# Where in SBUF the operands of the split-float matmuls start: taking a 64-byte pad out

## The chip, the cores and the metric

The kernel runs on one NeuronCore of a Trainium2 chip. The metric is the device time of one execution in microseconds. Three runs of the kernel before gave 1196.93, 1199.04 and 1201.48 us, so its median is 1199.04 us.

## The reference, cut to what matters

One decoder layer over 256 tokens of width 2048, batch 1, everything in float32:

```python
mod = silu(c) @ w_ada + b_ada                      # 2048 x 12288, six vectors of 2048
h = rms_norm(x, g) * (1 + scale_m) + shift_m
proj = h @ w_in                                    # 2048 x 5648: q, k, v, xs, z, B, C, dt
mix = concat(rms_norm(attention(q, k, v)), ssd(xs, z, B, C, dt)) @ w_out
x = x + gate_m * mix
h = rms_norm(x, g2) * (1 + scale_f) + shift_f
u = causal_dwconv(h @ w_up)                        # 2048 x 11264
x = x + gate_f * ((silu(u_g) * u_val) @ w_down)    # 5632 x 2048
return rms_norm(x, g3)
```

Attention is causal within one block of 256 tokens, with a bias per head and distance; the SSD part is one chunk of 256.

## The kernel before, in words

**Split floats.** Every large product is made of three float32r matmuls. A float32 number is kept as a high part (rounded to float32r) and a low part (the rest). `mm3` (L276 to L279) adds high x high, high x low and low x high. The tile of 128 x 128 weights is the operand that is loaded into TensorE (stationary), and the activations of 256 tokens stream past it: 256 columns, once the high half `a[:, 0:T]`, once the low half `a[:, T:2*T]`. Each matmul has its own weight load in front of it, so the program is one long sequence of pairs of a weight load and a matmul. The V projection (`v_unit`, L348) is turned round: there the activations are loaded and the weights stream, in pieces of 352, 352 and 336 columns.

**Weights.** SyncE's queue brings about 1 MB of weights at a time into a slot `s_...` of the pool `ws` (8320 bytes per partition a slot). `hi_lo_part` (L255 to L260) then makes two pieces of it: ScalarE writes the high part into a slot of the pool `wh` (L258), VectorE the low part into a slot of the pool `wl` (L259). Each of these pools has four slots of 4224 bytes. A unit of 2048 columns is two pieces of 1024, that is two runs of eight blocks, each block used by three matmuls.

**Activations.** What streams lies in `hT` (16 tiles of 2 x 256 numbers, for the input projection, tile names hT), `cat` and `cats` (for the output projection), `h2` (for the up projection, shown as h) and `gT` (for the down projection, shown as g). All are split floats, made by `hilo` or `ada_norm`.

**Stages.** Up to about 455 us: the modulation vectors (`ada`, partly on VectorE at L210, partly as float32 matmuls at L217 that lie between the others), the input projection (wa), attention, SSD (L557 to L562 are its small float32r matmuls, tile sg) and the output projection (oa). Their order is written out by hand in `ORDER`. After that the feed-forward: up projection over the first half of the contraction (u1a), then the second half (u2a) with the convolution and gate, down projection (da), then the other half of the columns (ua, da), and the last norm. In the feed-forward TensorE has nothing but `mm3`, except for a few matmuls at the end.

**Placement.** The pools are laid out in SBUF one behind the other in the order in which they are opened: `const`, `ws`, `pad0`, `wh`, `wl`, `pad1`, `tmp`, `xres`, `mix`, and so on. A pad is a pool with one tile of 16 floats, 64 bytes per partition, that nothing uses:

```python
    mkpool("pad0").tile([P, 16], F32, name="pad0")
    whp = mkpool("wh", 4)
    wlp = mkpool("wl", 4)
    mkpool("pad1").tile([P, 16], F32, name="pad1")
    tp = mkpool("tmp", 2)
```

Since 8320 is 65 x 128 and 4224 is 33 x 128, all slots of a pool start at the same place within 128 bytes, and the four slots of `wh` and of `wl` start in turn at 0 and 128 within 256 bytes.

Of the kernel before, what the change touches and what calls it, by code (L numbers as in the profile page):

```python
# [10 lines left out]
F32 = mybir.dt.float32  # L11
# [5 lines left out]
P = 128  # L17
# [77 lines left out]
def hymba_layer(ctx, tc, xT, c_row, cT, w_ada, vecs, consts, relb, onehot, w_vdt, w_in, w_out, w_up1, w_up, w_dn, outT):  # L95
# [3 lines left out]
    def mkpool(name, bufs=1, **kw):  # L99
        return ctx.enter_context(tc.tile_pool(name=name, bufs=bufs, **kw))  # L100
# [4 lines left out]
    mkpool("pad0").tile([P, 16], F32, name="pad0")  # L105
    whp = mkpool("wh", 4)
    wlp = mkpool("wl", 4)
    mkpool("pad1").tile([P, 16], F32, name="pad1")
    tp = mkpool("tmp", 2)
    xp = mkpool("xres")  # L110
    psp = mkpool("psum", 5, space=bass.MemoryType.PSUM)
# [805 lines left out]
```

## Time and profile before

| | |
|---|---|
| three runs | 1196.93, 1199.04, 1201.48 us |
| the profiled execution | 1196.57 us, span 1194.8 us |
| TensorE matmul busy | 1167.5 us, 98% of the span |
| TensorE weight load busy | 1113.3 us, 93% |
| VectorE, ScalarE busy | 915.0 us, 636.9 us |
| mean granted TensorE clock | 0.988 |
| read from HBM | 306 MB, 258 GB/s over the span |

Matmuls overlap each other in the records: one is shown as lasting 0.28 us although the next one starts after 0.11 us. So the rate of TensorE is read from the distance between the starts of neighbouring matmuls, called the gap here, or from how many of them a stretch of time holds.

### The profile page before, as it was taken

The page shows a single profiled execution, that of the slowest core. Times are in us where ns is not written, and L with a number is a line of the kernel's source. Part 1 is how long each engine was busy: PE and PEld are TensorE (multiplying, and loading weights), DVE is VectorE, ACT ScalarE, POOL GpSimd, SP SyncE. Part 2 cuts the span into 40 slices and gives each one's busy share as a digit, 9 for nine tenths or more (in the row PEclk, how much of TensorE's full clock was granted, in tenths as well). Part 3 has the DMA queues.
Part 4 walks back from the last instruction along what each step waited for, and adds up shares of the span by engine and source line. Part 5 has one row for each costly group of instructions (what it writes and reads, how often), then busy time and mean ns, then how long its engine had stood idle before and what let it go on. Part 6 is the DMA issues. An engine that isn't in the chain of part 4 may idle for free.

```text
span 1194.8 us, 23406 instructions
## 1 busy us (share of the span) xinstructions
PE 1167.5 (98%) x9760; PEld 1113.3 (93%) x9760; DVE 915.0 (77%) x1371; ACT 636.9 (53%) x959; POOL 0.9 (0%) x7
## 2 busy tenths in 40 slices
PE   6999999999999999999999999999999999999996
PEld 3899989988878898999999999999999999999995
DVE  6889979987988798786599984446888889656554
ACT  4544434457786544446567654444555555555552
POOL 0000000000000000000000000000000000000000
PEclk8899999999999999999999999999999999999998
DMA  9989988776765996997565545558878776545552
GB/s 359 409 338 337 327 335 304 276 268 246 287 242 214 365 383 237 343 357 245 183 204 186 201 146 194 195 194 276 295 299 301 284 282 227 196 150 196 194 194 96
DMA packets 47444, 309.60 MB, mean 259 GB/s; under 512 B 5568, under 2 KB 6761, under 8 KB 16105
## 3 DMA queue, kind: packets, MB, share of 16 engines
q1 hardware_dynamic: 46170, 307.04, 70.6%
q8 instruction: 76, 1.25, 0.4%
q10 hardware_dynamic: 1168, 1.06, 0.4%
q14 instruction: 30, 0.25, 0.1%
HBM read 305.98 MB, written 2.11 MB: 258 GB/s over the span
## 4 chain that ended last, share of the span: by engine, by line
PE 96%; DVE 1%; DMA 1%; ACT 1%; SPq 0%; issue 0%; DVEq 0%; ACTq 0%
PE ua L278 7%; PE ua L279 7%; PE da L279 7%; PE da L278 7%; PE da L277 7%; PE ua L277 7%; PE wa L277 6%; PE wa L279 6%; PE wa L278 6%; PE va L348 4%; PE u1a L278 3%; PE u1a L279 3%; PE u1a L277 3%; PE u2a L277 3%; PE u2a L279 3%; PE u2a L278 3%
## 5 line engine op out<-in xcount | busy, mean ns | idle before, releaser
L258 ACT CAST h_u<-s_u 128x1024 fp32r<-128x1024 f32 x176 | 183.6, 1050 | 188.3 <-PE ua L278 95.2
L259 DVE TENSOR_TENSOR l_u<-s_u,h_u 128x1024 fp32r<-128x1024 f32 x176 | 213.4, 1223 | 66.6 <-ACT h_u L258 64.6
L277 PE MATMUL ua<-h,h_u 128*128 128x256 f32 x704 | 194.3, 276 | 0.0
L278 PE MATMUL ua<-h,h_u 128*128 128x256 f32 x704 | 194.3, 276 | 0.0
L279 PE MATMUL ua<-h,l_u 128*128 128x256 f32 x704 | 194.3, 276 | 0.0
L279 PE MATMUL da<-g,l_d 128*128 128x256 f32 x704 | 194.3, 276 | 0.0
L278 PE MATMUL da<-g,h_d 128*128 128x256 f32 x704 | 194.3, 276 | 0.0
L277 PE MATMUL da<-g,h_d 128*128 128x256 f32 x704 | 194.1, 276 | 0.0
L259 DVE TENSOR_TENSOR l_d<-s_d,h_d 128x1024 fp32r<-128x1024 f32 (+1 forms) x128 | 108.8, 888 | 83.6 <-ACT h_d L258 83.6
L277 PE MATMUL wa<-hT,h_w 128*128 128x256 f32 x576 | 162.1, 282 | 0.8 <-ACT h_w L258 0.8
L279 PE MATMUL wa<-hT,l_w 128*128 128x256 f32 x576 | 159.8, 279 | 0.0
L278 PE MATMUL wa<-hT,h_w 128*128 128x256 f32 x576 | 159.7, 278 | 0.0
L258 ACT CAST h_d<-s_d 128x1024 fp32r<-128x1024 f32 (+1 forms) x128 | 98.2, 782 | 115.0 <-PE da L278 104.3
L210 DVE SCALAR_TENSOR_TENSOR ada<-ada,cb 128x2048 f32<-128x2048 f32 x60 | 137.2, 2288 | 11.5 <-DMA ada<-w_ada 11.2
L279 PEld LDWEIGHTS da<-g,l_d 128*128 128x128 f32 x704 | 132.2, 188 | 0.0
L277 PEld LDWEIGHTS ua<-h,h_u 128*128 128x128 f32 x704 | 132.2, 188 | 0.0
L278 PEld LDWEIGHTS ua<-h,h_u 128*128 128x128 f32 x704 | 132.2, 188 | 0.0
L279 PEld LDWEIGHTS ua<-h,l_u 128*128 128x128 f32 x704 | 132.2, 188 | 0.0
L278 PEld LDWEIGHTS da<-g,h_d 128*128 128x128 f32 x704 | 132.2, 188 | 0.0
L277 PEld LDWEIGHTS da<-g,h_d 128*128 128x128 f32 x704 | 132.1, 188 | 0.0
L258 ACT CAST h_w<-s_w 128x1024 fp32r<-128x1024 f32 x72 | 73.7, 1048 | 88.3 <-PE wa L278 42.7
L277 PEld LDWEIGHTS wa<-hT,h_w 128*128 128x128 f32 x576 | 108.4, 188 | 11.3 <-ACT h_w L258 3.6
(236 smaller groups left out, 2689.4 us busy)
## 6 DMA issues: line engine op xcount, KB each, us to landing
ada<-w_ada SPq DMA_DIRECT2D x96, 1024.0 KB, 6.1
s_u<-w_up SPq DMA_DIRECT2D x88, 1024.0 KB, 5.0
s_d<-w_dn SPq DMA_DIRECT2D x64, 704.0 KB, 4.1
s_w<-w_in SPq DMA_DIRECT2D x36, 1024.0 KB, 7.1
s_o<-w_out SPq DMA_DIRECT2D x16, 1024.0 KB, 8.3
s_v<-w_vdt SPq DMA_DIRECT2D x8, 1040.0 KB, 6.6
x<-xT SPq DMA_DIRECT2D x4, 512.0 KB, 4.8
outT<-x SPq DMA_DIRECT2D x2, 640.0 KB, 3.0
```

The lines of the kernel that those rows point to most:

```text
L210: dve.scalar_tensor_tensor(ws[:, :D], ws[:, :D], 1.0, cb, op0=ALU.mult, op1=ALU.mult, accum_out=mod[:, j:j + 1])
L258: act.copy(wh[:, :m], ws[:, o:o + m])
L259: dve.tensor_sub(wl[:, :m], ws[:, o:o + m], wh[:, :m].bitcast(F32))
L277: pe.matmul(o, whs, a[:, 0:T], start=first, stop=False)
L278: pe.matmul(o, whs, a[:, T:2 * T], start=False, stop=False)
L279: pe.matmul(o, wls, a[:, 0:T], start=False, stop=last)
L348: pe.matmul(va[tt][i][:, :n], lo if st == 2 else hi, (wl if st == 1 else wh)[:, s], start=f and st == 0, stop=l and st == 2)
```

## The change

The pool `pad1` is no longer opened. Everything opened after it moves down by 64 bytes per partition; everything before it stays. No instruction is added, removed or moved: on each engine the built program has the same instructions on the same tiles in the same order.

```diff
     mkpool("pad0").tile([P, 16], F32, name="pad0")
     whp = mkpool("wh", 4)
     wlp = mkpool("wl", 4)
-    mkpool("pad1").tile([P, 16], F32, name="pad1")
     tp = mkpool("tmp", 2)
     xp = mkpool("xres")
```

Where the tiles start in the built program, in bytes of a partition, with the rest after division by 256 in brackets:

| tiles | before | after |
|---|---|---|
| slots of wh | 60672 (0), 64896 (128), 69120 (0), 73344 (128) | the same |
| slots of wl | 77568 (0), 81792 (128), 86016 (0), 90240 (128) | the same |
| three slots of ws | 35648 (64), 43968 (192), 52288 (64) | the same |
| tri_r and ones_r, loaded for sg | 33216 (192), 33728 (192) | the same |
| hT, first tile | 137536 (64) | 137472 (0) |
| cat, cats, first tiles | 170304 (64), 137536 (64) | 170240 (0), 137472 (0) |
| h2 | 125248 (64) | 125184 (0) |
| gT, first tile | 174400 (64) | 174336 (0) |
| am, streams for sg | 153920 (64) | 153856 (0) |
| x, and the first scratch tile of tmp | 108864 (64), 94528 (64) | 108800 (0), 94464 (0) |
| ada and s slots beside ws, first | 203200 (192) | 203136 (128) |

The tiles within hT, cat, cats, h2 and gT are steps of 2048 bytes with two halves of 1024, so each of their streams starts at the same rest.

## Rows read from the trace of the kernel before

**Rows 1.** The page's part 1: busy time, share of the span, instructions.

```profile
PE 1167.5 (98%) x9760; PEld 1113.3 (93%) x9760; DVE 915.0 (77%) x1371; ACT 636.9 (53%) x959; POOL 0.9 (0%) x7
```

**Rows 2.** The page's part 4: shares of the chain that ended last.

```profile
PE 96%; DVE 1%; DMA 1%; ACT 1%; SPq 0%; issue 0%; DVEq 0%; ACTq 0%
```

**Rows 3.** Stretches: PE, PEld, DVE, ACT, POOL busy, PEclk, DMA share, GB/s.

```profile
36.90:100.00 63.10, 62.27 (x513) 58.02 (x512) 54.75 (x81) 35.02 (x50) 0.00 (x0) 1.00 0.94 364
100.00:228.00 128.00, 128.00 (x1044) 123.35 (x1044) 113.86 (x153) 51.08 (x56) 0.00 (x0) 1.00 0.86 313
228.00:454.70 226.70, 225.99 (x1770) 193.36 (x1772) 186.77 (x376) 141.70 (x271) 0.00 (x0) 1.00 0.74 283
464.20:465.30 1.10, 1.10 (x7) 1.10 (x7) 1.10 (x1) 0.00 (x0) 0.00 (x0) 0.50 0.41 171
588.60:1088.60 500.00, 500.00 (x4414) 500.00 (x4413) 381.70 (x548) 279.69 (x402) 0.00 (x0) 1.00 0.65 225
```

**Rows 4.** Groups of matmuls of L277 by shape; L278 and L279 have the same counts.

```profile
L277 PE MATMUL ua<-h,h_u 128*128 128x256 f32 x704 | 194.3, 276 | 0.0
...
L277 PE MATMUL da<-g,h_d 128*128 128x256 f32 x704 | 194.1, 276 | 0.0
L277 PE MATMUL wa<-hT,h_w 128*128 128x256 f32 x576 | 162.1, 282 | 0.8 <-ACT h_w L258 0.8
...
L277 PE MATMUL u2a<-h,h_u 128*128 128x256 f32 x352 | 97.2, 276 | 0.0
...
L277 PE MATMUL u1a<-h,h_u 128*128 128x256 f32 x352 | 96.5, 278 | 0.7 <-ACT h L313 0.7
...
L277 PE MATMUL oa<-cat,h_o 128*128 128x256 f32 x128 | 36.6, 286 | 0.0
...
L277 PE MATMUL oa<-cats,h_o 128*128 128x256 f32 x128 | 35.8, 280 | 0.0
```

**Rows 5.** TensorE in order of time, 36 to 1182 us: start, lasting (us).

```profile
36.89 0.31 PE L277 MATMUL wa<-hT,h_w 128*128 128x256 f32 x1
...
588.69 0.28 PE L277 MATMUL u2a<-h,h_u 128*128 128x256 f32 x1
...
1088.49 0.28 PE L277 MATMUL da<-g,h_d 128*128 128x256 f32 x1
...
1181.54 0.28 PE L279 MATMUL da<-g,l_d 128*128 128x256 f32 x1
```

**Rows 6.** TensorE in order of time, 156 to 160 us, around a stretch of wide gaps.

```profile
156.24 0.61 PE L217 MATMUL adp<-ada,c 128*32 128x512 f32 x4
156.79 0.39 PE L277 MATMUL wa<-hT,h_w 128*128 128x256 f32 x1
157.01 0.28 PE L278 MATMUL wa<-hT,h_w 128*128 128x256 f32 x1
...
159.49 0.28 PE L278 MATMUL wa<-hT,h_w 128*128 128x256 f32 x1
159.60 0.28 PE L279 MATMUL wa<-hT,l_w 128*128 128x256 f32 x1
159.72 0.28 PE L277 MATMUL wa<-hT,h_w 128*128 128x256 f32 x1
159.83 0.28 PE L278 MATMUL wa<-hT,h_w 128*128 128x256 f32 x1
```

**Rows 7.** The chain that ended last, a piece of the V projection.

```profile
170.43 11.40 PE va L348 x72
```

**Rows 8.** TensorE in order of time, SSD's matmuls.

```profile
350.94 0.28 PE L559 MATMUL sg<-am,ones_r 128*128 128x256 f32 x1
...
351.41 0.28 PE L277 MATMUL oa<-cat,h_o 128*128 128x256 f32 x1
```

**Rows 9.** TensorE in order of time, start of the feed-forward, at the half clock.

```profile
464.32 0.41 PE L278 MATMUL u1a<-h,h_u 128*128 128x256 f32 x1
...
465.18 0.41 PE L277 MATMUL u1a<-h,h_u 128*128 128x256 f32 x1
```

## The prediction

> **What bounds the kernel now.** I read the page's busy times first [rows 1]: TensorE's matmuls cover 98% of the span, VectorE 77%, ScalarE 53%. The chain that ended last says the same from the other side: 96% of it is TensorE [rows 2]. The stretches then show that this is no average over unlike stages [rows 3]: from 36.9 us on TensorE is busy nearly without a break, in the feed-forward for all of 500 us, while VectorE has 118 us of those 500 free and the DMA share is 0.65. So nearly all of the time is a number of matmuls times the gap between them, and the change can matter only if it alters the gap.
>
> The number is fixed: three lines of `mm3` with 704, 704, 576, 352, 352, 128 and 128 matmuls each [rows 4], 8,832 in all, the first at 36.89 us and the last at 1181.54 us [rows 5]. The V projection adds 288.
>
> The gap has two levels. From 588.69 to 1088.49 us there are 4,410 gaps in 499.80 us [rows 5], 113.33 ns each: the **narrow level**. Between 157.01 and 159.72 us there are 23 gaps in 2.71 us, 117.8 ns each, and the next gap is again 0.11 us [rows 6]: the **wide level**, 4.5 ns more. I took the starts of all 8,832 one by one. The gaps behind them: 7,622 narrow, 113.3 on average, 1,101 wide at 117.9, and 109 longer ones, where something stands between. All but 1 of the wide ones begin before 470 us; from the full clock at about 465 us to the end 6,307 gaps are narrow.
>
> Neither level is the bare rate. The granted clock is 1.00, the upper of the two levels (2.4 GHz), in the long stretch [rows 3]; 256 columns at one a cycle would take 106.7 ns. The narrow gap is a sixteenth more.
>
> **Does the start address have a hand in it?** This is what the change turns on, and three readings bear on it. I set the address table of the change beside the starts.
>
> First, how a stretch of wide gaps begins and ends. It begins when other matmuls have come between, as the modulation matmuls at 156.24 us do [rows 6]. Of 30 such restarts with weights in a slot at rest 0 (within 256 bytes), 28 began wide; of 9 at rest 128, 5. Such a stretch ended, without any pause, only where the weights pass on to another slot: at 20 of 24 passages into rest 128, the one at 159.72 us among them [rows 6], and at none of 5 passages into rest 0. The streams start at rest 64 throughout. So wide or narrow is not decided by load alone; the distance from the weights to the stream (64 or 192 bytes within 256) goes with it.
>
> Second, the only streams that lie at multiples of 128 already are those of the V projection, where wh and wl stream and the activations are loaded. A piece of 72 matmuls takes 11.40 us [rows 7], 158.3 ns each. At the narrow level's rate per column (113.33 / 256 = 0.443 ns), the mean of 352, 352 and 336 columns would take 153.5. That is 4.8 ns more a matmul: the wide level, in a stretch of 72 with hardly a narrow gap among them.
>
> Third, SSD's matmuls have both operands off the multiples, 128 bytes apart within 256. From 350.94 to 351.41 us there are four gaps in 0.47 us [rows 8], 117.5 ns: wide as well, though they always come just after an interruption, so they say less.
>
> **The change, part by part.** No instruction changes, so nothing is queued differently and no wait is added.
>
> *The streams of `mm3`* go from rest 64 to rest 0. The distance to the weights becomes 0 or 128 instead of 64 or 192, and every stream starts at a multiple of 128, as in the V projection. No row shows this pair. The bounds: nothing, if the narrow level holds as it does now; and the wide level for every narrow gap, 7,622 x 4.5 = 34.3 us, or with the V projection's 4.8 ns 36.6 us. Below nothing, a gain: the 1,101 wide gaps become narrow, 5.0 us. I take the wide level, because both rows that are nearest in placement (V for the stream's own rest, sg for the distance of 128) show it, and I take it for the feed-forward alone, 6,307 x 4.5 = 28.4 us. The 1,315 narrow gaps before that (5.9 us more) I leave at nothing: there the gaps are mixed already, restarts decide afresh every few microseconds, and DMA shares of 0.74 to 0.94 [rows 3] leave pauses that take some of it up. They stay in the upper end.
>
> *The V projection's loaded operand* goes from rest 64 to 0, its stream stays. Its gaps are wide now; at best 288 x 4.8 = 1.4 us come back. I take 0.
>
> *VectorE and ScalarE* get x, the scratch tiles and the destinations of `hilo` 64 bytes lower. Cost nothing: it is hidden under TensorE, which is busy 500 of 500 us while VectorE needs 381.7 and ScalarE 279.7 [rows 3]. Their work would have to grow by 31% before TensorE waited; in the tightest stretch, 100 to 228 us, by 12% (113.86 of 128).
>
> *DMA* lands in the ada and s slots beside `ws` 64 bytes lower, and so does x. The three main slots stay. The only stretch where that could show has a DMA share of 0.94 over 63.1 us [rows 3]; one per cent there would be 0.6 us either way. I take 0.
>
> The sum is +28.4 us. The profiled execution took 1196.57 us, 2.47 below the median 1199.04; on the median it gives **1227.4 us**.
>
> **A rule against it.** The skill's own rule on SBUF gives no reason for any difference: the Trainium skill, page "SBUF — State Buffer", section "Specifications (TRN2)", gives cachelines of 16 bytes, and 64 bytes are four whole lines, so by that page the sum would be 0. The passages by slot above do not agree with a period as short as 16 bytes.
>
> **The rivals.**
>
> *Nothing changes.* The narrow level, once reached, lasted for 6,307 gaps while the weights' slots alternated between two distances, so it may be indifferent to the other two distances as well, and the V projection may have wide gaps because of its 352 and 336 columns. Against it stand the 20 of 24 and 0 of 5. Time: 1199, within about 5 us, as the mixed stretch may shift a little.
>
> *The wide level goes (faster).* If a stream at rest 0 restarts with narrow gaps after each interruption, before 455 us, all 1,101 wide gaps and the V projection come back: 5.0 + 1.4 = 6.4 us, 1192.6 us. It decides itself at the first restarts, from 37 us on. For it speaks that restarts at one distance are quicker than at the other already; against it the V rows.
>
> *The stream itself gets quicker.* If the sixteenth were the price of starting at rest 64, every gap would fall, at most to 106.7 ns: 8,723 x 6.6 = 58 us at most, so between 1141 and about 1180 us. Against it: at the half clock (0.50, 1.2 GHz [rows 3]) four gaps from 464.32 to 465.18 us take 0.86 us [rows 9], 215 ns against 213.3 for 256 columns, so the same placement has no such price there; and the few narrow gaps of the V projection, with streams at rest 0, keep that rate (18 gaps of 155 to 156 ns behind 352 columns). The Trainium skill, page "TensorE: Matmul & The Clock Gate", section "Back-to-back issue gap", gives columns / 2.4 + 2.5 ns, 109.2 ns here; the trace's 113.3 does not agree with it, and if placement were the reason the estimate by that page would be 36 us off the time.
>
> *Half of it.* Within the forecast case the wide level may hold only for the slots at one distance: 14.2 us, 1213 us.
>
> **How the numbers follow.** Wide level in the feed-forward 0.45, with 1213 to 1237 as its own range (half the slots; everything at the V projection's 4.8 ns). Nothing changes 0.33. The wide level goes 0.15. The stream gets quicker 0.07. About 0.5%, 6.0 us, is what a measurement here can tell from no change. The gain of 6.4 us lies on that edge; I count 0.10 of its 0.15 as faster. Faster: 0.10 + 0.07 = 0.17. Same: 0.33 + 0.05 = 0.38. Slower: 0.45. The range goes from 1192, which takes in the 6.4 us, to 1237; it leaves out the quicker stream and little else.
>
> **What would show it.** Right: the stretch of 500 us in the feed-forward holds about 4,245 matmuls instead of 4,414, their mean duration goes from 276 to about 279 ns, the span grows by some 28 us and all of it after 465 us, with VectorE's and ScalarE's mean durations unchanged. Half right: a gap that alternates with the slots. Wrong: 4,414 matmuls again in that stretch. If the time grows without a change of gap, the cause is a wait, and my reading of the whole change is wrong.

## The result, and the profile after

Four runs of the changed kernel gave 1240.95 to 1242.36 us, median 1241.38, beside 1198.57 (1196.93 to 1201.48, four runs) for the kernel before. The ratio is 1.0362, 95% interval 1.0346 to 1.0379. The change costs 42.8 us. The prediction was 1227.4 with a range to 1237: the sign was right, the size a third too small.

The profiled execution took 1241.74 us, its span is 1240.0 us. TensorE is as full as before and fills 45 us more with the same 9,760 matmuls; VectorE and ScalarE are busy for as long as they were [rows 1, 2]. First the page's part 1, then its part 4:

```profile
PE 1212.7 (98%) x9760; PEld 1158.7 (93%) x9760; DVE 917.6 (74%) x1371; ACT 636.0 (51%) x959; POOL 0.9 (0%) x7
...
PE 95%; DVE 2%; DMA 1%; ACT 1%; issue 0%; SPq 0%; DVEq 0%; ACTq 0%
```

The stretches of the changed kernel, with the columns of [rows 3] (PE, PEld, DVE, ACT, POOL busy, PEclk, DMA share, GB/s); all but the third, the whole feed-forward, answer to rows there:

```profile
36.20:100.00 63.80, 62.97 (x505) 58.70 (x505) 53.75 (x81) 34.21 (x48) 0.00 (x0) 1.00 0.94 361
100.00:228.00 128.00, 128.00 (x1012) 123.32 (x1011) 110.38 (x149) 50.30 (x54) 0.00 (x0) 1.00 0.83 305
...
468.20:1226.80 758.60, 756.94 (x6344) 756.52 (x6345) 525.32 (x722) 389.48 (x555) 0.00 (x0) 1.00 0.62 218
588.60:1088.60 500.00, 500.00 (x4196) 500.00 (x4196) 367.34 (x518) 262.64 (x374) 0.00 (x0) 1.00 0.62 218
```

In the same 500 us of the feed-forward TensorE now starts 4,196 matmuls where it started 4,414. It is busy for all 500 both times, at a granted clock of 1.00 both times, and VectorE and ScalarE have more free time than before. So nobody waits for anybody: the matmuls themselves stand further apart. In 100 to 228 us it is 1,012 for 1,044, so the loss begins before the feed-forward.

By the starts of single matmuls: the first one of the feed-forward moved from 460.1 to 468.2 us (+8.1), and from there to the start of its last `mm3` matmul it takes 758.6 us instead of 721.5 (+37.1). Those two make up the 45.2 us by which the span grew. The mean gaps went from 115.3 to 119.1 ns in the input projection, from 115.6 to 119.05 in the output projection and from 113.34 to 119.23 in the feed-forward; V's from 158.35 to 159.07. Of all 8,832, only 812 are under 115.5 ns; 566 of these are in the feed-forward, 563 of them in slots at rest 128, where the gaps vary (below).

The groups of matmuls of the first line of `mm3` (L276 here, L277 before [rows 4]) show the same, a little hidden, as a matmul's duration in the records holds the overlap too: 282 and 283 ns for 276 in the feed-forward.

```profile
L276 PE MATMUL da<-g,h_d 128*128 128x256 f32 x704 | 198.8, 283 | 0.0
L276 PE MATMUL ua<-h,h_u 128*128 128x256 f32 x704 | 198.7, 282 | 0.0
...
L276 PE MATMUL wa<-hT,h_w 128*128 128x256 f32 x576 | 164.6, 286 | 0.8 <-ACT h_w L257 0.8
...
L276 PE MATMUL oa<-cat,h_o 128*128 128x256 f32 x128 | 37.1, 290 | 0.0
...
L276 PE MATMUL oa<-cats,h_o 128*128 128x256 f32 x128 | 36.4, 284 | 0.0
```

The two operations that make the weights' halves keep their durations (1050 and 1223 ns in the kernel before). From the page's part 5:

```profile
L257 ACT CAST h_u<-s_u 128x1024 fp32r<-128x1024 f32 x176 | 183.4, 1048 | 213.2 <-PE ua L277 113.0
L258 DVE TENSOR_TENSOR l_u<-s_u,h_u 128x1024 fp32r<-128x1024 f32 x176 | 214.0, 1223 | 93.7 <-ACT h_u L257 91.3
```

And the new gap alternates with the weights' slot. TensorE in order of time in the changed kernel, at three passages from one slot to the next:

```profile
900.63 0.28 PE L276 MATMUL ua<-h,h_u 128*128 128x256 f32 x1
900.75 0.28 PE L277 MATMUL ua<-h,h_u 128*128 128x256 f32 x1
...
903.51 0.28 PE L276 MATMUL ua<-h,h_u 128*128 128x256 f32 x1
...
906.35 0.28 PE L276 MATMUL ua<-h,h_u 128*128 128x256 f32 x1
```

At 900.63 us the weights pass into a slot at rest 0, at 903.51 into one at rest 128, at 906.35 into one at rest 0 again. A slot holds 24 matmuls: 2.88 us for the first 24, 120.0 ns each, and 2.84 us for the second, 118.3. The first level is exact (of the 1,056 gaps in such slots of the matmuls ua, 1,050 are 120 ns), the second is a mean of gaps between 112 and 124. Neither is the wide level of before, 117.8.

### The profile page after: what moved, and what is told of

Read it like the earlier page. It is cut to its first block, busy times and chain, and to the rows that moved or that the text cites. A ratio compares the mean times of both kernels' runs of the same rounds, so it can differ in the third digit from the quotient of the medians.

```text
span 1240.0 us, 23406 instructions
## 1 busy us (share of the span) xinstructions
PE 1212.7 (98%) x9760; PEld 1158.7 (93%) x9760; DVE 917.6 (74%) x1371; ACT 636.0 (51%) x959; POOL 0.9 (0%) x7
## 4 chain that ended last, share of the span: by engine, by line
PE 95%; DVE 2%; DMA 1%; ACT 1%; issue 0%; SPq 0%; DVEq 0%; ACTq 0%
PE da L278 7%; PE da L276 7%; PE ua L278 7%; PE ua L276 7%; PE ua L277 7%; PE da L277 7%; PE wa L276 6%; PE wa L278 6%; PE wa L277 6%; PE va L347 4%; PE u2a L278 3%; PE u2a L276 3%; PE u2a L277 3%; PE u1a L277 3%; PE u1a L278 3%; PE u1a L276 3%
## 5 line engine op out<-in xcount | busy, mean ns | idle before, releaser
L258 DVE TENSOR_TENSOR l_u<-s_u,h_u 128x1024 fp32r<-128x1024 f32 x176 | 214.0, 1223 | 93.7 <-ACT h_u L257 91.3
L278 PE MATMUL da<-g,l_d 128*128 128x256 f32 x704 | 198.8, 282 | 0.0
L276 PE MATMUL da<-g,h_d 128*128 128x256 f32 x704 | 198.8, 283 | 0.0
L276 PE MATMUL ua<-h,h_u 128*128 128x256 f32 x704 | 198.7, 282 | 0.0
L278 PE MATMUL ua<-h,l_u 128*128 128x256 f32 x704 | 198.6, 282 | 0.0
L277 PE MATMUL da<-g,h_d 128*128 128x256 f32 x704 | 198.3, 282 | 0.0
L277 PE MATMUL ua<-h,h_u 128*128 128x256 f32 x704 | 198.3, 282 | 0.0
L276 PE MATMUL wa<-hT,h_w 128*128 128x256 f32 x576 | 164.6, 286 | 0.8 <-ACT h_w L257 0.8
L278 PE MATMUL wa<-hT,l_w 128*128 128x256 f32 x576 | 162.2, 283 | 0.0
L277 PE MATMUL wa<-hT,h_w 128*128 128x256 f32 x576 | 162.0, 282 | 0.0
L278 PEld LDWEIGHTS da<-g,l_d 128*128 128x128 f32 x704 | 134.4, 191 | 0.0
L277 PEld LDWEIGHTS da<-g,h_d 128*128 128x128 f32 x704 | 134.3, 191 | 0.0
L276 PEld LDWEIGHTS da<-g,h_d 128*128 128x128 f32 x704 | 134.3, 191 | 0.0
L278 PEld LDWEIGHTS ua<-h,l_u 128*128 128x128 f32 x704 | 133.9, 190 | 0.0
L277 PEld LDWEIGHTS ua<-h,h_u 128*128 128x128 f32 x704 | 133.8, 190 | 0.0
L276 PEld LDWEIGHTS ua<-h,h_u 128*128 128x128 f32 x704 | 133.8, 190 | 0.0
L276 PEld LDWEIGHTS wa<-hT,h_w 128*128 128x128 f32 x576 | 109.4, 190 | 11.2 <-ACT h_w L257 3.6
```

The costliest lines, as they stand in the source:

```text
L258: dve.tensor_sub(wl[:, :m], ws[:, o:o + m], wh[:, :m].bitcast(F32))
L276: pe.matmul(o, whs, a[:, 0:T], start=first, stop=False)
L277: pe.matmul(o, whs, a[:, T:2 * T], start=False, stop=False)
L278: pe.matmul(o, wls, a[:, 0:T], start=False, stop=last)
```

## The experiments

All kernels below have the matmuls and weight loads of the kernel before; only addresses differ. "Distance" is the stream's start minus the weights' start within 256 bytes, so the kernel before has 64 and 192 in turn, the changed one 0 and 128. Gaps are means after 500 us unless said otherwise.

**1. Both pads out.** The weights' slots go to rest 192 and 64, the streams to 192. Every address differs from the changed kernel's by 64 bytes, and the distance is the same.

```diff
-    mkpool("pad0").tile([P, 16], F32, name="pad0")
     whp = mkpool("wh", 4)
     wlp = mkpool("wl", 4)
-    mkpool("pad1").tile([P, 16], F32, name="pad1")
```

> Both pads gone: the slots of wh and wl start at 192 and 64 within 256 bytes, all streams of mm3 at 192, so no stream is at a multiple of 128, but the distance from the weights to the stream is 0 or 128, as after the change. Theory A (the distance within 256 bytes sets the gap: 113.3 ns at 64 and 192, 120.0 at 0, about 118.2 at 128): 1241 us, gap 120.0 behind weights in slots at 192 and about 118.2 in slots at 64. Theory B (the stream's own start at a multiple of 128 is what costs): 1199 us, gap 113.3. Theory C (weights at a multiple of 128 are needed as well as streams off it): over 1199 with a gap that does not follow the distance.

Measured: 1241.77 us, beside 1196.81 for the kernel before on that chip. The long stretch of the feed-forward:

```profile
588.60:1088.60 500.00, 500.00 (x4196) 500.00 (x4195) 367.35 (x518) 262.94 (x374) 0.00 (x0) 1.00 0.63 218
```

The same 4,196 matmuls as in the changed kernel, and in the up projection the same two levels: 120.00 ns for slots at the stream's own rest, 118.33 for those 128 bytes off. None of its `mm3` streams and none of its weights lies at a multiple of 128, and the loss is complete.

**2. Only the first pad out.** The streams go to rest 0, as in the changed kernel; the weights to 192 and 64, so the distance is 64 and 192, as in the kernel before.

```diff
-    mkpool("pad0").tile([P, 16], F32, name="pad0")
     whp = mkpool("wh", 4)
     wlp = mkpool("wl", 4)
     mkpool("pad1").tile([P, 16], F32, name="pad1")
```

> pad0 gone, pad1 kept: weights at 192 and 64 within 256 bytes, streams at 0, a multiple of 128 as after the change, distance 64 or 192 as before it. Theory A (distance): 1199 us and 113.3 ns. Theory B (the stream's own start at a multiple of 128): about 1241 us and 118 to 120 ns.

Measured: 1199.24 us, a mean gap of 113.4 ns in the feed-forward.

```profile
588.60:1088.60 500.00, 500.00 (x4412) 500.00 (x4412) 381.42 (x546) 279.56 (x401) 0.00 (x0) 1.00 0.65 225
```

Streams at multiples of 128 cost nothing if the weights stand at the right distance. With the first experiment this settles it for moves of 64 bytes: the distance between the two operands decides, not where either of them starts.

**3. The changed kernel, with a pad ahead of the feed-forward's tiles.** h2 and gT go back to rest 64, so the feed-forward has the distance of before and all that lies ahead of it keeps the changed addresses.

```diff
+    mkpool("pad2").tile([P, 16], F32, name="pad2")
     fp = mkpool("ffn")
```

> The changed kernel with the 64 bytes put back just ahead of the feed-forward's own pools: h2, d0 and gT are where they were before the change; x, the scratch tiles, hT, cat and the s slots beside ws stay 64 bytes lower. Theory A (distance of weights and streams): the feed-forward's gap is 113.3 again and the part up to it stays about 8 us longer than before, so 1206 to 1208 us. Theory D (what costs is x, the scratch or the slots, through ScalarE, VectorE or DMA writing elsewhere): about 1241 us, feed-forward gap above 118.

Measured: 1209.95 us. Two stretches, up to the feed-forward and within it:

```profile
36.20:467.00 430.80, 429.35 (x3352) 384.66 (x3350) 359.24 (x611) 229.35 (x379) 0.00 (x0) 1.00 0.79 297
588.60:1088.60 500.00, 500.00 (x4414) 500.00 (x4414) 378.94 (x540) 277.93 (x397) 0.00 (x0) 1.00 0.64 225
```

The feed-forward has its 4,414 matmuls again, though x, the scratch tiles and the slots beside `ws` lie where the change put them. Of what the pad moves, matmuls read h2 and gT alone, so it is the streams that cost the feed-forward its time. The feed-forward begins at 467.8 us, as late as in the changed kernel: the first 8 us are lost ahead of it. This one run came out 2 to 4 us above what was expected, within the spread of the kernel before (1195.43 to 1202.09 us in 23 runs); waits can account for most of it. Total, count and longest wait in us:

```profile
PE u1a L278 <- DVE l_u L258: 2.7, 4, 0.8
```

The kernel before has no such wait: here TensorE, at narrow gaps again after a late start, catches up with VectorE.

**4. The second pad at 128 bytes.** The streams go to rest 128 and the weights stay at 0 and 128, so the two distances change places among the slots. It asks whether the period is 128 or 256.

```diff
-    mkpool("pad1").tile([P, 16], F32, name="pad1")
+    mkpool("pad1").tile([P, 32], F32, name="pad1")
```

> pad1 of 128 bytes: weights at 0 and 128 within 256 bytes, streams at 128, so the two distances 0 and 128 are exchanged between the slots. Theory A with a period of 256 bytes: about 1241 us, with 120.0 ns now behind weights in the slots at 128 and the uneven 118.2 ns in the slots at 0. Theory A with a period of 128 bytes and the slots themselves being different: 120.0 ns still in the slots at 0. Theory B (multiple of 128): also about 1241 us.

Measured: 1240.75 us. The long stretch:

```profile
588.60:1088.60 500.00, 500.00 (x4202) 500.00 (x4201) 367.81 (x518) 262.81 (x374) 0.00 (x0) 1.00 0.63 218
```

TensorE in order of time at the passages into a slot at rest 0 (900.17 us), rest 128 (903.01) and rest 0:

```profile
900.17 0.28 PE L277 MATMUL ua<-h,h_u 128*128 128x256 f32 x1
...
903.01 0.28 PE L277 MATMUL ua<-h,h_u 128*128 128x256 f32 x1
...
905.89 0.28 PE L277 MATMUL ua<-h,h_u 128*128 128x256 f32 x1
```

Now the 24 matmuls at rest 0 take 2.84 us and those at rest 128 take 2.88: the levels went over to the other slots with the distance. 0 and 128 are different distances, so a period of 128 bytes is out. A period of 512 is out as well: the first and the third slot of `wh` (60672 and 69120) differ by 33 x 256, so within 512 bytes they lie at different places, and in the changed kernel both have 120.0 ns.

**5. Only the low halves moved.** From the changed kernel: a pad of 64 bytes between `wh` and `wl`, and 48 floats behind `wl`, so the streams stay at rest 0. The high halves keep the distance 0 or 128, the low halves get 192 or 64. During each matmul the next one's weights are loaded (in the kernel before, the load for the L277 matmul of 900.13 us starts at 900.02 us, together with the L279 matmul ahead of it), so this asks which weights count, those in use or those being loaded.

```diff
     whp = mkpool("wh", 4)
+    mkpool("padl").tile([P, 16], F32, name="padl")
     wlp = mkpool("wl", 4)
+    mkpool("pad1").tile([P, 48], F32, name="pad1")
```

> From the changed kernel: 64 bytes ahead of wl alone, and 192 bytes behind it, so that the streams stay at 0 within 256 bytes, wh at 0 and 128 (distance 0 and 128), and wl is at 64 and 192 (distance 64 and 192). The three matmuls of mm3 load high, high, low weights. Theory A1 (the loading of the next weights and the running stream get in each other's way, so the gap behind a matmul goes with the weights of the next one): the second line of mm3 is near 113 ns, since low weights are loaded under it, the first and third stay at 118 to 120. Theory A2 (a matmul's own weights and its own stream): the third line is near 113 ns, the first and second stay. Both: about 1226 to 1231 us. Theory A3 (each slot keeps its gap whatever the distance): 1241 us.

Measured: 1222.63 us, 1197.60 for the kernel before beside it.

```profile
588.60:1088.60 500.00, 500.00 (x4277) 500.00 (x4277) 375.11 (x533) 269.03 (x385) 0.00 (x0) 1.00 0.62 220
```

A mean gap of 117.0 ns. By line and slot: the first line of `mm3` 118.2 (slot at rest 0) and 112.5 ns (rest 128), the second 117.4 and 118.3, the third, with the low weights, 118.6 and 115.7. No line has both slots narrow, and no line has in both slots what it had in the changed kernel. So the reading that only the weights in use count falls, and so does the one that only those being loaded count. The gap depends on the neighbours too, in a way that these numbers don't resolve.

**6 and 7. The second pad at 32 and 96 bytes.** Distances of 32 and 160, and of 96 and 224: is the gap a matter of steps of 64 bytes, or does it rise evenly?

```diff
-    mkpool("pad1").tile([P, 16], F32, name="pad1")
+    mkpool("pad1").tile([P, 8], F32, name="pad1")
```

> pad1 of 32 bytes: distances 32 and 160 within 256 bytes. Theory A with steps of 64 bytes (what counts is in which 64 bytes the two start): either as after the change, 1241 us with 120.0 and about 118.2 ns, or as before it, 1199 us with 113.3. Theory A with a smooth dependence: gaps between, some 115 to 118 ns, 1212 to 1230 us.

The other has `[P, 24]` in that place.

> pad1 of 96 bytes: distances 96 and 224. Theory A with steps of 64 bytes, counted from the weights: 96 as 64 and 224 as 192, 113.3 ns and 1199 us, if 32 and 160 are as 0 and 128; the other way round if 32 and 160 are as 64 and 192. Smooth: between, 1212 to 1230 us.

Measured: 1223.06 us with 32 bytes, 1241.05 with 96. The stretch, for 32 and then for 96:

```profile
588.60:1088.60 500.00, 500.00 (x4273) 500.00 (x4273) 374.48 (x532) 267.82 (x384) 0.00 (x0) 1.00 0.62 220
```

```profile
588.60:1088.60 500.00, 500.00 (x4196) 500.00 (x4195) 367.83 (x518) 262.27 (x374) 0.00 (x0) 1.00 0.61 218
```

Neither of the two shapes. A distance of 32 or 160 gives 116.6 and 117.5 ns, 96 and 224 give 119.9 and 118.4: on one side of 64 some 3 to 4 ns, on the other all of the loss.

**8. All weights at one distance.** Slots of 4352 bytes (17 x 256) instead of 4224, so all lie at rest 192, and all streams at rest 128: distance 192 everywhere. To make room, two small scratch tiles share the places of two others. If the distance of 64 is what starts the wide gaps of before, they should go.

```diff
-HU = 1056
+HU = 1088
...
-    mkpool("pad0").tile([P, 16], F32, name="pad0")
     whp = mkpool("wh", 4)
     wlp = mkpool("wl", 4)
-    mkpool("pad1").tile([P, 16], F32, name="pad1")
+    mkpool("pad1").tile([P, 48], F32, name="pad1")
...
-        s2 = mtmp("dt_s2", n, "dt4", 1)
+        s2 = mtmp("dt_s2", n, "dt1", 1)
...
-        r = mtmp("dt_r", n, "dt5", 1)
+        r = mtmp("dt_r", n, "dt2", 1)
```

> Slots of wh and wl of 4352 bytes, 17 x 256, so that all four of each start at 192 within 256 bytes, and pads that put the streams at 128: every stream of mm3 lies 192 bytes from its weights. Theory A, with what the trace before showed (stretches of wide gaps end only at passages into a slot at distance 192): the 1,089 wide gaps ahead of the feed-forward mostly go, 3 to 5 us, so 1194 to 1196 us. If the passage from slot to slot matters rather than the distance: 1199 us or more.

Measured: 1195.95 us beside 1197.60. The feed-forward is narrow (113.37 ns), and ahead of it there are 1,009 narrow gaps in the input projection and 338 in the output projection, against 949 and 366 in the kernel before, 1,347 together against 1,315: the wide gaps are not gone, and the 3 to 5 us that were expected did not come as forecast.

```profile
588.60:1088.60 500.00, 500.00 (x4414) 500.00 (x4414) 380.77 (x548) 279.52 (x402) 0.00 (x0) 1.00 0.63 224
```

**9 and 10. The up projection's streams at 48 and at 80 bytes.** The kernel before, with h2 cut out of a tile that is 64 floats longer. The distance is 48 or 176 in the up projection (then 80 or 208); the down projection, which reads gT, keeps 64 and 192 and so stands as a control in the same execution.

```diff
-    h2 = fp.tile([P, KT, 512], F32R, name="h2")
+    h2 = fp.tile([P, KT * 512 + 64], F32R, name="h2")[:, 60:60 + KT * 512].rearrange("p (k t) -> p k t", k=KT)
```

> The kernel before with h2 alone moved: its streams start at 48 within 256 bytes, so in the up projection (4,224 of the 6,336 matmuls of the feed-forward) the distance is 48 and 176, in the down projection 64 and 192 as before. A good place that is one point, with the gap rising evenly towards 32 (117.0 ns): 115 ns in the up projection, about 1206 us. A good place as wide as 64 bytes around 64: 113.3 ns, 1198 us. Only whole multiples of 64 are good: 117 ns or more, 1213 us or more.

The other cuts from element 4 on.

> The same with h2 at 80: distance 80 and 208 in the up projection. Even rise towards 96 (119.2 ns): 116 ns there, about 1210 us. A good place as wide as 64 bytes: 113.3 ns, 1198 us. Only multiples of 64: 117 ns or more, 1213 us or more.

Measured: 1218.62 and 1222.68 us, the kernel before 1197.85 in 23 runs. A stretch of the up and one of the down projection, first for the kernel before, then for 48, then for 80:

```profile
588.60:700.00 111.40, 111.40 (x986) 111.40 (x985) 106.18 (x185) 79.26 (x124) 0.00 (x0) 1.00 0.55 185
720.00:820.00 100.00, 100.00 (x884) 100.00 (x884) 45.03 (x53) 44.88 (x60) 0.00 (x0) 1.00 0.61 201
```

```profile
588.60:700.00 111.40, 111.40 (x940) 111.40 (x939) 100.64 (x169) 75.03 (x116) 0.00 (x0) 1.00 0.52 179
720.00:820.00 100.00, 100.00 (x885) 100.00 (x884) 45.59 (x54) 44.77 (x61) 0.00 (x0) 1.00 0.57 196
```

```profile
588.60:700.00 111.40, 111.40 (x934) 111.40 (x933) 98.95 (x166) 73.65 (x114) 0.00 (x0) 1.00 0.53 183
720.00:820.00 100.00, 100.00 (x885) 100.00 (x884) 46.16 (x56) 43.92 (x61) 0.00 (x0) 1.00 0.56 190
```

The down projection holds 884, 885 and 885 matmuls in 100 us; the up projection 986, 940 and 934 in 111.4. Sixteen bytes to either side of 64 lose it: 118.3 and 119.2 ns at 48 and 176, 119.9 and 119.3 at 80 and 208.

The mean gap by distance, from all the kernels so far:

| distance | gap, ns | distance | gap, ns |
|---|---|---|---|
| 0 | 120.00 | 128 | 118.33 |
| 32 | 116.6 | 160 | 117.5 |
| 48 | 118.3 | 176 | 119.2 |
| 64 | 113.33 | 192 | 113.33 |
| 80 | 119.9 | 208 | 119.3 |
| 96 | 119.9 | 224 | 118.4 |

The two distances of a row alternate within one execution, so the values of a row aren't quite independent: 192 is narrow by itself too (experiment 8), 64 by itself was not tried. Of the twelve, only 64 and 192 are narrow. In the rows that begin with 32, 48, 80 and 96 the streams themselves don't start at a multiple of 64 while the weights do, so a share of the stream's own place isn't ruled out there.

**11. Only the first pad out, timed.** The kernel of experiment 2 again: does it beat the kernel before?

> Weights at 192 and 64, streams at 0, timed. Theory A (distance 64 and 192 is what makes 113.3 ns, wherever both lie): the same as before within 0.5%. If the absolute place of either has a share of its own: over 0.5% away.

Measured: 1197.57 us median (12 runs) against 1197.85 (23 runs), ratio 1.0001, interval 0.9987 to 1.0014. The same: moving both operands by 64 bytes together changes nothing.

**12. All weights at one distance, timed.** The kernel of experiment 8 again.

> All slots at distance 192, timed, since one look gave 1195.95 us beside 1197.6. If the wide gaps ahead of the feed-forward depend on which of the two good distances is met: 3 to 5 us less than before. If they only follow the interruptions: within 2 us of before.

Measured: of 14 executions eleven took 1194.21 to 1208.3 us and three 1221.66 to 1223.96; the ratio of 1.0017 (0.9998 to 1.0037) leaves out these three. So the expected 3 to 5 us don't come. One of the three was profiled, and within that one trace both levels occur. Two stretches of it, up to 539 us and from 541 us on, then the long one:

```profile
466.40:539.00 72.60, 72.60 (x642) 72.60 (x642) 56.01 (x56) 33.42 (x40) 0.00 (x0) 1.00 0.89 335
541.00:700.00 159.00, 159.00 (x1353) 159.00 (x1352) 129.43 (x203) 100.66 (x150) 0.00 (x0) 1.00 0.54 189
...
588.60:1088.60 500.00, 500.00 (x4247) 500.00 (x4247) 374.21 (x533) 266.52 (x383) 0.00 (x0) 1.00 0.61 218
```

642 matmuls in 72.6 us are 113.1 ns each; 1,353 in 159 us are 117.5, and 4,247 in 500 us are 117.7. The granted clock is 1.00 on both sides. Between the two stretches TensorE, in order of time, shows this:

```profile
538.96 0.28 PE L276 MATMUL u1a<-h,h_u 128*128 128x256 f32 x1
539.07 0.28 PE L277 MATMUL u1a<-h,h_u 128*128 128x256 f32 x1
539.79 0.39 PE L278 MATMUL u1a<-h,l_u 128*128 128x256 f32 x1 [0.44 <-DVE l_u L258]
540.02 0.28 PE L276 MATMUL u1a<-h,h_u 128*128 128x256 f32 x1
```

One start comes 0.72 us after the one before it, because VectorE's low half was late. The 637 gaps ahead of it are narrow; the 5,660 behind it are wide to the end of the feed-forward (117.8 ns). The addresses and the clock are the same on both sides, so a change of address isn't needed for a change of level. In experiment 8 the same kernel waited less at the same matmul, and the gaps were narrow again after two wide ones. First its stretch from 541 us on, then the matmuls around the wait:

```profile
541.00:700.00 159.00, 159.00 (x1405) 159.00 (x1405) 133.70 (x216) 104.13 (x156) 0.00 (x0) 1.00 0.56 194
...
539.05 0.28 PE L277 MATMUL u1a<-h,h_u 128*128 128x256 f32 x1
539.24 0.39 PE L278 MATMUL u1a<-h,l_u 128*128 128x256 f32 x1
539.46 0.28 PE L276 MATMUL u1a<-h,h_u 128*128 128x256 f32 x1
```

There the start comes 0.19 us after the one before it, and 1,405 matmuls follow in the stretch where the other execution has 1,353. In experiments 2 and 3, where slots alternate between 64 and 192, starts that came 0.8 to 1.1 us after the one before, in the same part of the up projection, were followed by narrow gaps at once, or by wide ones up to one of the next passages into a slot at distance 192, unless another late start came first: they have 6,218 and 6,115 narrow gaps in the feed-forward. So alternating distances may be what lets the kernel before return; that is read from these few cases and was not tested by itself. No version here beats it.

## Why the prediction was right in kind and too small

**The bound, and what could change.** Right. TensorE's 8,832 matmuls times their gap is the time; the whole loss is in the gap, no wait is behind it, and VectorE, ScalarE and DMA cost nothing at their new addresses (experiment 3 has them there, and its feed-forward is narrow).

**Two reasons for the wide level: half right.** The prediction took it "because both rows that are nearest in placement (V for the stream's own rest, sg for the distance of 128) show it". The distance was the true one. The stream's own rest was not: streams at rest 0 are narrow in experiment 2 and streams off the multiples are wide in experiment 1. For the slots at distance 0 V was the only row, so that half of the forecast was right by luck; for those at 128 it rested on four gaps. V's gaps [rows 7] were read as a sign of a stream at rest 0; they were wide before, are wide after (the 72 matmuls take 11.48 us instead of 11.40), and lie between 158.0 and 159.3 ns at every distance tried. They were no evidence. From the chain of waits of the changed kernel:

```profile
173.67 11.48 PE va L347 x72
```

Taking nothing for V's loaded operand was right.

**The mis-sized term.** "I take it for the feed-forward alone, 6,307 x 4.5 = 28.4 us." The count was right, the price was not: the gaps there grew by 5.9 ns, and 6,329 x 5.9 = 37.3 us. That is 8.9 us of the miss. 120.0 and 118.3 ns are levels of their own, which stand in no row of the trace before, as nothing in it had this pair of distances for longer than four gaps [rows 8]. The upper bound used the same two wide levels (its own terms, 1199.04 + 36.6, give 1235.6 and not 1237), and that is why the range ended 4 us too low. An unseen state was priced with the nearest seen one, and the nearest was not an upper bound.

**The term left at nothing.** "The 1,315 narrow gaps before that (5.9 us more) I leave at nothing." They cost 8.1 us: 1,676 gaps of the input projection by 3.8 ns are 6.3 us and 728 of the output projection by 3.5 are 2.5, together 8.8. The first of these matmuls started 0.74 us earlier than before (36.15 for 36.89 us [rows 5]), which leaves 8.1, so next to nothing was absorbed on the way. That the pauses there would take some of it up failed: from 100 to 228 us TensorE is busy 128.00 of 128 us, and wherever it is, every nanosecond counts. Here the wide gaps grew too, to the new levels. The first of the matmuls in the changed kernel:

```profile
36.15 0.41 PE L276 MATMUL wa<-hT,h_w 128*128 128x256 f32 x1
```

The two terms together are 17 us more than forecast. Measured against one profiled execution the growth is 45.2 us, by the medians 42.8, as the profiled execution of the kernel before lay 2 us below its median.

**The signs.** 4,245 matmuls were expected in the long stretch and 279 ns of duration, 4,196 and 282 to 283 came: the right signs, at the larger size. "All of it after 465 us" was wrong by the 8.1 us. "A gap that alternates with the slots" came too, but both of its levels are wide, so it meant no half of the loss.

**The rivals.** Nothing changes, the gaps get narrow, the stream gets quicker: all refuted by 120.0 and 118.3 ns. The first was backed by the rule that SBUF's lines are 16 bytes (the Trainium skill, page "SBUF — State Buffer", section "Specifications (TRN2)"). A stream that is moved by 16 bytes takes up as many such lines as before, so by that rule nothing would change; experiments 9 and 10 do not agree with that as far as TensorE's rate goes, since a distance of 48 or 80 instead of 64 costs 5 to 6.5 ns a matmul. The evidence that spoke against this rival, 20 of 24 passages against 0 of 5, was the strongest reading in the prediction, and it deserved more than the 0.45 given to the forecast. (It is a little less clean than that: behind one passage into rest 0, at 88.59 us, the gaps turn narrow after three more, where the order of the lines changes.)

**What stays open.** Why 64 and 192 alone are narrow; whether the stream's own place has a share where it isn't a multiple of 64; how the weights in use and those being loaded share in it (experiment 5); what makes a late start end on the wide level (experiments 8 and 12); and why V's gaps are wide at every distance.

## What to carry to other kernels

When TensorE is busy without a break, read the gap between matmul starts before anything else: if float32r products of 256 columns stand at more than 113.3 ns apart at the full clock, look at the distance between the two operands' start addresses within 256 bytes, and try 64 and 192 in turn. Neatly aligned tiles are the slowest case here (120.0 ns at distance 0), and an edit that adds or drops a tile in SBUF can cost 3.6% without changing one instruction. A wait of under a microsecond may cost far more than itself if it leaves the engine on a wider level, as in one execution here (0.72 us, then 5,660 wide gaps); with slots that alternate between 64 and 192 every execution profiled got back to narrow gaps.

## What the runs showed of the hardware that was not expected

The gaps look quantised. At the upper clock (2.4 GHz) 256 columns at one a cycle are 106.67 ns; the narrow gap of 113.33 is 17/16 of that, and the 120.00 at distance 0 is 18/16. At the lower (1.2 GHz) the kernel before shows no such addition:

```profile
463.26:465.82 2.56, 2.56 (x14) 2.56 (x14) 2.56 (x6) 0.51 (x1) 0.00 (x0) 0.50 0.54 227
...
463.26 0.41 PE L279 MATMUL u1a<-h,l_u 128*128 128x256 f32 x1
...
465.82 0.38 PE L279 MATMUL u1a<-h,l_u 128*128 128x256 f32 x1
```

From 463.26 to 465.82 us there are 12 gaps at a granted clock of 0.50, 213.3 ns each, which is 256 columns at one a cycle. The 215 ns that the prediction took from four gaps [rows 9] came from the rounding of the two times. The levels between (116.6 to 119.9) are means over uneven gaps.

The rate depends on both operands' addresses together, with a period of 256 bytes, though each of them starts on a multiple of 16 bytes in every kernel here, and moving both by 64 bytes changes nothing (1197.57 against 1197.85 us, and 1241.77 against 1241.38).

At one and the same distance two levels hold themselves, 113.3 and 117.8 ns: 637 gaps of the one and then 5,660 of the other, with a single wait between them, in one execution (experiment 12).
